# Scores of two heads in one two-bank tile, in a decoder step of attention, state space and MLP layers

## The chip, the cores and the metric

The kernel runs on one core of a Trainium2 chip. The metric is the device time of one execution in microseconds, as the median of several runs; a profiled execution gives the trace that is read here. The core has a matrix engine (TensorE, PE in the rows, with its weight loads as PEld), a vector engine (DVE), an activation engine (ACT), GpSimd (POOL) and a sync engine (SP); SP and POOL issue most transfers.

## The reference

One step of a trunk of two layers is computed for two groups with the same weights: a prompt of 512 rows without past, and a sample of 8 sequences of 8 rows, each with 2,048 cached keys and values per head. The first layer is stick-breaking attention with 16 heads of 64, the second a diagonal state-space layer; each is followed by an MLP with a convolution. For the change only the attention of the prompt counts:

```python
z = einsum("bqhd,bkhd->bhqk", q, k) * HEAD_DIM ** -0.5 + bias[h]
causal = k_pos < q_pos
log_keep = where(causal, log_sigmoid(-z), 0)
between = cumsum(log_keep, reverse) - log_keep
weights = where(causal, exp(log_sigmoid(z) + between), 0)
out = einsum("bhqk,bkhd->bqhd", weights, v)
```

The kernel computes it in products: the running product of sigmoid(-z) from the right, times sigmoid(z).

## The kernel before

The prompt's 512 rows are four tiles of 128 rows (NT = 4). Heads are handled in pairs: the 128 columns of a pair c are head 2c (partitions 0 to 63 once transposed) and head 2c + 1 (partitions 64 to 127).

The loop at L786 to L797 runs over c from 0 to 9, with three stages of different pairs in each turn. `project_pair` computes keys and values of pair c by matmuls of 256 columns (L266 to L268, psg). `norm_pair` (L631) normalizes queries and keys of pair c - 1 and transposes them on TensorE into PSUM tiles pqk (L651), which ACT and DVE copy to qkT. `prompt_pair` (L661) does the attention of pair c - 2. In turns 8 and 9 there is no projection.

A fourth stream of work, `sample_cache`, reads 64 pairs of cache pages per run. A step of it is 1 MB of keys (kp, issued on POOL, turned by DVE at L427), 1 MB of values (vp, issued on SP), 32 passes of scores (z, L448), sigmoids and scans, two transposes (L473) and 16 passes of value sums (po, L483). It yields four times per step. After the stream the sample's own new rows follow (`sample_new`: zn at L522, pon at L559), then its output projection (pso), and then the sample joins the prompt in the MLP.

How these are woven: `tick(cycles)` is called where matmuls are issued. Each companion (the stream with a period of 2,400 cycles, `norm_pair` with 6,000, `prompt_pair` with 1,200) is advanced by one yield when its period is used up; a companion doesn't count its own ticks. That gives the order in which instructions are written down. The framework then arranges them for each engine by that priority and by when they can be ready, with a modelled time, and each engine runs its own list strictly in that arranged order. So an instruction of later priority may stand ahead of one that would have to wait.

In `prompt_pair` an item is one row tile i and one head e. For each item: one score matmul (L674; float32, two passes each with its own weight load), a mask matmul in bfloat16 onto the diagonal block (L675), two sigmoids on ACT (L678, L679), a scan and a product on DVE (L681, L682). One item later its weights are transposed back into the same PSUM tile z (L691) and copied by ACT to pwT (L693). Two items later, for both heads of a row, the value sums go into poT (L704). The tiles z and pqk share two PSUM buffers of one bank each (tag "pz", PZ = 2). The tiles pleft, psg and pwT have two buffers each. PSUM's eight banks are taken: two for pz, two for the projections, one for poT, three for the stream.

Of the kernel before, what the change touches and what calls it, by code (L numbers as in the profile page):

```python
# [9 lines left out]
F32 = mybir.dt.float32  # L10
# [3 lines left out]
AF = mybir.ActivationFunctionType  # L14
# [3 lines left out]
P = 128  # L18
D = 1024
KC = D // P  # L20
SEQ = 512
NT = SEQ // P
# [5 lines left out]
HD = 64  # L28
# [21 lines left out]
PZ, PG = 2, 2  # L50
# [40 lines left out]
def hybrid_kernel(  # L91
# [9 lines left out]
    V, S, G, T, SP = nc.vector, nc.scalar, nc.gpsimd, nc.tensor, nc.sync  # L101
# [10 lines left out]
    ident = const.tile([P, P], F32, name="ident")  # L112
# [184 lines left out]
    def attention_layer(sp, sps):  # L297
# [333 lines left out]
        def norm_pair(pool, psp, c, k, v):  # L631
# [14 lines left out]
            out = []  # L646
            for m in range(2):
                yield
                ps = psp.tile([P, SEQ], F32, name="pqk", tag="pz", bufs=PZ)
                for i in range(NT):  # L650
                    T.transpose(ps[:, i * P:(i + 1) * P], k[:, i] if m else q_all[:, c, i], ident)  # L651
                a = pool.tile([P, SEQ], F32, name="qkT", tag=f"qkT{m}")
                if m:
                    V.tensor_copy(a, ps)
                else:
                    S.activation(a, ps, AF.Copy, scale=qgT)
                out.append(a)
# [3 lines left out]
        def prompt_pair(pool, psp, c, qT, kT, v):  # L661

            po = psp.tile([P, SEQ], F32, name="poT", tag="poT", bufs=1)
            items = [(i, e) for i in range(NT) for e in range(2)]
            live = {}
            for x in range(len(items) + 2):
                if x < len(items):
                    i, e = items[x]
                    nk = (i + 1) * P
                    h = 2 * c + e  # L670
                    r = slice(e * HD, e * HD + HD)

                    z = psp.tile([P, SEQ], F32, name="pz", tag="pz", bufs=PZ)
                    T.matmul(z[:, :nk], qT[r, i * P:nk], kT[r, :nk], start=True, stop=False)  # L674
                    T.matmul(z[:, i * P:nk], ident_b, mask_b, start=False, stop=True)  # L675
                    left = pool.tile([P, SEQ], F32, name="pleft", tag="pleft", bufs=B1)
                    sg = pool.tile([P, SEQ], F32, name="psg", tag="psg", bufs=B2)
                    S.activation(left[:, :nk], z[:, :nk], AF.Sigmoid, bias=nbias_h[:, h:h + 1], scale=-0.125)  # L678
                    S.activation(sg[:, :nk], z[:, :nk], AF.Sigmoid, bias=bias_h[:, h:h + 1], scale=0.125)  # L679
                    back = left[:, :nk][:, ::-1]  # L680
                    V.tensor_tensor_scan(back, back, back, 1.0, ALU.mult, ALU.min)  # L681
                    V.tensor_tensor(sg[:, :nk - 1], sg[:, :nk - 1], left[:, 1:nk], ALU.mult)  # L682
                    live[x] = z, sg
                    tick(4 * nk + P)
                    yield
                if x - 1 in live:
                    z, sg = live[x - 1]
                    i = items[x - 1][0]
                    nk = (i + 1) * P
                    for kb in range(i + 1):  # L690
                        T.transpose(z[:, kb * P:(kb + 1) * P], sg[:, kb * P:(kb + 1) * P], ident)  # L691
                    wT = pool.tile([P, SEQ], F32, name="pwT", tag="pwT", bufs=B3)
                    S.copy(wT[:, :nk], z[:, :nk])  # L693
                    live[x - 1] = wT
                    tick(2 * nk)
                    yield
                if x - 2 in live and x % 2:

                    i = items[x - 2][0]
                    wTs = [live.pop(y) for y in (x - 3, x - 2)]  # L700
# [6 lines left out]
                    yield  # L707
# [3 lines left out]
        with pool_(name="start", bufs=2) as wp, pool_(name="start_ps", bufs=5, space=PSUM) as psp:  # L711
# [9 lines left out]
            with tc.high_priority():  # L721
# [4 lines left out]
                for n in range(2):  # L726
                    ps = bank()
# [1036 lines left out]
```

## Time and profile before

| | us |
|---|---|
| median of three runs | 1748.3 |
| lowest and highest of them | 1742.35, 1749.19 |
| profiled execution | 1757.19 |
| its span, first to last instruction | 1755.2 |
| TensorE busy in it | 1657.5 (94%) |
| DVE busy | 1156.4 (66%) |
| ACT busy | 739.3 (42%) |
| GpSimd busy | 379.0 (22%) |

TensorE's mean granted clock was 0.976 of full speed, and 297.4 MB were moved in the span, 169 GB/s on average, over 300 GB/s while the cache is streamed. Busy shares over the whole span mix stages with different limits, so a stage is read by itself: busy time of each engine, granted clock and DMA share in its window, then what ends the waits there.

### The profile page before, as it was taken

How to read it: one execution, taken by the hardware profiler on the slowest of the kernel's cores; microseconds unless marked ns; L12 is line 12 of the kernel's file. 1: busy time of each engine (PE TensorE's matmuls, PEld its weight loads, DVE VectorE, ACT ScalarE, POOL GpSimd, SP SyncE). 2: the span in 40 equal slices, each digit the busy share in tenths (PEclk: the TensorE clock that was granted, in tenths of full speed). 3: DMA queues.
4: the chain of work that ended last, by engine and by line, in shares of the span. 5: the costliest groups of instructions: out<-in, count | busy, mean ns of one | idle time of the engine just before them, and what ended most of it. 6: DMA issues, size and time to landing. Idle time of an engine off the chain costs nothing. (4 is left out here: it accounts for less than half of the span.)

```text
span 1755.2 us, 34213 instructions
## 1 busy us (share of the span) xinstructions
PE 1657.5 (94%) x12765; PEld 1405.2 (80%) x12765; DVE 1156.4 (66%) x2132; ACT 739.3 (42%) x1526; POOL 379.0 (22%) x583
## 2 busy tenths in 40 slices
PE   5999999999898899989998999999999999999999
PEld 4877776665577769868898897898889989999897
DVE  8377888888778668977687777655456444444343
ACT  4344555555533643323445354544434323323231
POOL 4032333332332002652242330111101001000000
PEclk8999999998899999989999999999999999999999
DMA  8299989898798444234757364544322222222221
GB/s 272 72 313 316 316 284 340 288 344 287 253 346 292 147 131 124 96 110 110 163 147 188 117 170 123 156 163 137 103 69 83 81 85 85 82 77 86 82 87 56
DMA packets 278714, 297.44 MB, mean 169 GB/s; under 512 B 70808, under 2 KB 214129, under 8 KB 278548
## 3 DMA queue, kind: packets, MB, share of 16 engines
q1 hardware_dynamic: 240210, 226.65, 41.8%
q0 software_dynamic: 37184, 67.55, 11.2%
q8 instruction: 101, 1.65, 0.4%
q10 hardware_dynamic: 1154, 1.05, 0.2%
q14 instruction: 65, 0.53, 0.1%
HBM read 268.93 MB, written 26.13 MB: 168 GB/s over the span
## 5 line engine op out<-in xcount | busy, mean ns | idle before, releaser
L139 DVE TENSOR_TENSOR wlo<-raw,whi 128x1024 fp32r<-128x1024 f32 x203 | 255.6, 1261 | 256.2 <-ACT whi L138 241.3
L880 PE MATMUL up<-hT,whi 128*128 128x256 f32 (+2 forms) x1344 | 408.0, 304 | 12.0 <-DVE gf L1000 6.3
L881 PE MATMUL up<-hT,whi 128*128 128x256 f32 (+2 forms) x1344 | 403.9, 301 | 0.0
L882 PE MATMUL up<-hT,wlo 128*128 128x256 f32 (+2 forms) x1344 | 403.8, 301 | 0.0
L138 ACT CAST whi<-raw 128x1024 fp32r<-128x1024 f32 x206 | 215.4, 1049 | 337.7 <-PE up L881 155.3
L880 PEld LDWEIGHTS up<-hT,whi 128*128 128x128 f32 x1344 | 257.9, 192 | 21.5 <-DVE gf L1000 8.0
L881 PEld LDWEIGHTS up<-hT,whi 128*128 128x128 f32 x1344 | 258.0, 192 | 3.5 <-issue 0.8
L882 PEld LDWEIGHTS up<-hT,wlo 128*128 128x128 f32 x1344 | 257.6, 192 | 1.3
L415 POOL DMA_DIRECT2D kp<-in_cache_k_dram x256 | 166.1, 649 | 360.8 <-DVE kt L427 190.9
L427 DVE STREAM_TRANSPOSE kt<-kp 128x1024 f32<-128x1024 f32 x128 | 152.1, 1222 | 42.2 <-DMA kp<-in_cache_k_dram 20.6
L986 POOL COPY cst<-apad 128x2 f32<-128x2 f32 x44 | 39.0, 885 | 517.2 <-ACT apad L974 517.2
L266 PE MATMUL dn<-whi,g 128*128 128x512 f32 x352 | 136.9, 399 | 7.8 <-DVE xres L1077 5.0
L267 PE MATMUL dn<-wlo,g 128*128 128x512 f32 x352 | 140.5, 399 | 0.0
L268 PE MATMUL dn<-whi,g 128*128 128x512 f32 x352 | 139.1, 398 | 0.0
L266 PE MATMUL psg<-whi,hT 128*128 128x256 f32 (+1 forms) x320 | 100.7, 317 | 0.1
L267 PE MATMUL psg<-wlo,hT 128*128 128x256 f32 (+1 forms) x320 | 99.3, 311 | 0.0
L268 PE MATMUL psg<-whi,hT 128*128 128x256 f32 (+1 forms) x320 | 98.0, 309 | 0.0
L457 ACT ACTIVATE left<-z,nbias_r 128x128 f32<-128x128 f32 x128 | 40.3, 367 | 111.1 <-PE z L448 109.9
L266 PEld LDWEIGHTS dn<-whi,g 128*128 128x128 f32 x352 | 66.1, 189 | 24.6 <-DVE xres L1077 5.5
L483 PE MATMUL po<-vp,wT 128*32 128x256 f32 x1024 | 73.4, 404 | 9.5 <-DMA vp<-in_cache_v_dram 7.3
L268 PEld LDWEIGHTS dn<-whi,g 128*128 128x128 f32 x352 | 66.5, 189 | 15.5 <-DVE g L1016 0.3
L267 PEld LDWEIGHTS dn<-wlo,g 128*128 128x128 f32 x352 | 66.6, 189 | 15.3
(484 smaller groups left out, 3291.4 us busy)
## 6 DMA issues: line engine op xcount, KB each, us to landing
kp<-in_cache_k_dram POOLq DMA_DIRECT2D x256, 256.0 KB, 6.5
vp<-in_cache_v_dram SPq DMA_DIRECT2D x128, 512.0 KB, 7.0
raw<-in_ffn_w_up_dram SPq DMA_DIRECT2D x96, 512.0 KB, 4.4
raw<-in_ffn_w_down_dram SPq DMA_DIRECT2D x48, 512.0 KB, 3.3
raw<-in_attn_w_qkv_dram SPq DMA_DIRECT2D x64, 128.0 KB, 6.4
raw<-in_attn_w_o_dram SPq DMA_DIRECT2D x16, 512.0 KB, 5.4
raw<-in_ssm_w_glu_dram SPq DMA_DIRECT2D x32, 256.0 KB, 3.1
f_scr<-ca SPq DMA_DIRECT2D x8, 512.0 KB
```

The lines of the kernel that those rows point to most:

```text
L138: S.copy(hi, src)
L139: eng.tensor_tensor(lo, src, hi.bitcast(F32), ALU.subtract)
L266: T.matmul(ps, x[0], whi, start=st, stop=False)
L267: T.matmul(ps, x[0], wlo, start=False, stop=False)
L268: T.matmul(ps, x[1], whi, start=False, stop=sp_)
L415: last_dma[G] = G.dma_start(kps[i][32 * x:32 * x + 32], page[j])
L427: V.transpose(kts[i, a].rearrange("p b c k -> p b (c k)"), kps[i][:, :, a * 256:(a + 1) * 256])
L457: S.activation(left[:, a, :P], z[:, a * P:(a + 1) * P], AF.Sigmoid, bias=nbias_r[:, a:a + 1], scale=-0.125)
L483: T.matmul(po[32 * h:32 * h + 32, a].rearrange("p (s j d) -> p s j d", s=2, j=2), wT[:, a, 32 * h:32 * h + 32], v[:, a, h], start=m0 == NP ...
L880: T.matmul(ps[:, :t1 - t0], w[0][:, k, :], hi, start=k == 0, stop=False)
L881: T.matmul(ps[:, :t1 - t0], w[0][:, k, :], lo, start=False, stop=False)
L882: last_mm["PE"] = T.matmul(ps[:, :t1 - t0], w[1][:, k, :], hi, start=False, stop=k == KC - 1)
```

## The change

The two one-bank buffers of the tag "pz" become one buffer of two banks, a tile of 128 x 2 x 512. In `norm_pair` queries and keys are transposed into the two halves of one such tile, with one yield ahead of both in place of one ahead of each. In `prompt_pair` the loop goes over row tiles: the score matmuls of both heads are issued one behind the other, then both masks, then sigmoids, scan and product of each head, then after three yields (with the value sums of the row before between them) the transposes and copies of both heads. The ticks of a row were 2 x (4 nk + 128) + 2 x 2 nk + 4 nk, with nk = 128 (i + 1), and are now (4 nk + 256) + 4 nk + 4 nk. Nothing else changes.

```diff
--- before.py
+++ after.py
@@ -47,7 +47,7 @@
 ASTEPS, AEND = 44, 20
 SSTART = 14
 GROUPS = [[4], [0, 1], [2, 3]]
-PZ, PG = 2, 2
+PG = 2
 LAG = 19000
 GLAG = 6
 GT = 3
@@ -644,16 +644,16 @@
             with tc.high_priority():
                 SP.dma_start(k_out[:, c * P:(c + 1) * P].rearrange("(i p) f -> p i f", p=P), k)
             out = []
+            yield
+            ps = psp.tile([P, 2, SEQ], F32, name="pqk", tag="pz", bufs=1)
             for m in range(2):
-                yield
-                ps = psp.tile([P, SEQ], F32, name="pqk", tag="pz", bufs=PZ)
                 for i in range(NT):
-                    T.transpose(ps[:, i * P:(i + 1) * P], k[:, i] if m else q_all[:, c, i], ident)
+                    T.transpose(ps[:, m, i * P:(i + 1) * P], k[:, i] if m else q_all[:, c, i], ident)
                 a = pool.tile([P, SEQ], F32, name="qkT", tag=f"qkT{m}")
                 if m:
-                    V.tensor_copy(a, ps)
+                    V.tensor_copy(a, ps[:, m])
                 else:
-                    S.activation(a, ps, AF.Copy, scale=qgT)
+                    S.activation(a, ps[:, m], AF.Copy, scale=qgT)
                 out.append(a)
             ready[c] = *out, v
             yield
@@ -661,50 +661,53 @@
         def prompt_pair(pool, psp, c, qT, kT, v):
 
             po = psp.tile([P, SEQ], F32, name="poT", tag="poT", bufs=1)
-            items = [(i, e) for i in range(NT) for e in range(2)]
-            live = {}
-            for x in range(len(items) + 2):
-                if x < len(items):
-                    i, e = items[x]
-                    nk = (i + 1) * P
+            sums = None
+            for i in range(NT):
+                nk = (i + 1) * P
+
+                z = psp.tile([P, 2, SEQ], F32, name="pz", tag="pz", bufs=1)
+                for e in range(2):
+                    r = slice(e * HD, e * HD + HD)
+                    T.matmul(z[:, e, :nk], qT[r, i * P:nk], kT[r, :nk], start=True, stop=False)
+                for e in range(2):
+                    T.matmul(z[:, e, i * P:nk], ident_b, mask_b, start=False, stop=True)
+                sgs = []
+                for e in range(2):
                     h = 2 * c + e
-                    r = slice(e * HD, e * HD + HD)
-
-                    z = psp.tile([P, SEQ], F32, name="pz", tag="pz", bufs=PZ)
-                    T.matmul(z[:, :nk], qT[r, i * P:nk], kT[r, :nk], start=True, stop=False)
-                    T.matmul(z[:, i * P:nk], ident_b, mask_b, start=False, stop=True)
                     left = pool.tile([P, SEQ], F32, name="pleft", tag="pleft", bufs=B1)
                     sg = pool.tile([P, SEQ], F32, name="psg", tag="psg", bufs=B2)
-                    S.activation(left[:, :nk], z[:, :nk], AF.Sigmoid, bias=nbias_h[:, h:h + 1], scale=-0.125)
-                    S.activation(sg[:, :nk], z[:, :nk], AF.Sigmoid, bias=bias_h[:, h:h + 1], scale=0.125)
+                    S.activation(left[:, :nk], z[:, e, :nk], AF.Sigmoid, bias=nbias_h[:, h:h + 1], scale=-0.125)
+                    S.activation(sg[:, :nk], z[:, e, :nk], AF.Sigmoid, bias=bias_h[:, h:h + 1], scale=0.125)
                     back = left[:, :nk][:, ::-1]
                     V.tensor_tensor_scan(back, back, back, 1.0, ALU.mult, ALU.min)
                     V.tensor_tensor(sg[:, :nk - 1], sg[:, :nk - 1], left[:, 1:nk], ALU.mult)
-                    live[x] = z, sg
-                    tick(4 * nk + P)
-                    yield
-                if x - 1 in live:
-                    z, sg = live[x - 1]
-                    i = items[x - 1][0]
-                    nk = (i + 1) * P
+                    sgs.append(sg)
+                tick(4 * nk + 2 * P)
+                yield
+                if sums:
+                    sums()
+                yield
+                yield
+                wTs = []
+                for e, sg in enumerate(sgs):
                     for kb in range(i + 1):
-                        T.transpose(z[:, kb * P:(kb + 1) * P], sg[:, kb * P:(kb + 1) * P], ident)
+                        T.transpose(z[:, e, kb * P:(kb + 1) * P], sg[:, kb * P:(kb + 1) * P], ident)
                     wT = pool.tile([P, SEQ], F32, name="pwT", tag="pwT", bufs=B3)
-                    S.copy(wT[:, :nk], z[:, :nk])
-                    live[x - 1] = wT
-                    tick(2 * nk)
-                    yield
-                if x - 2 in live and x % 2:
-
-                    i = items[x - 2][0]
-                    wTs = [live.pop(y) for y in (x - 3, x - 2)]
+                    S.copy(wT[:, :nk], z[:, e, :nk])
+                    wTs.append(wT)
+                tick(4 * nk)
+                yield
+
+                def sums(i=i, wTs=wTs):
+
                     for kb in range(i + 1):
                         for e, wT in enumerate(wTs):
                             r = slice(e * HD, e * HD + HD)
                             T.matmul(po[r, i * P:(i + 1) * P], v[:, kb, r], wT[:, kb * P:(kb + 1) * P],
                                      start=kb == 0, stop=kb == i)
                     tick(4 * (i + 1) * P)
-                    yield
+            sums()
+            yield
             S.copy(q_all[:, c].rearrange("p i f -> p (i f)"), po)
 
         xT = columns_tile()
```

## Rows read from the trace of the kernel before

**Rows 1.** Stages: window, busy us and instructions per engine, TensorE clock, DMA share, GB/s.
```profile
130.00:412.00 282.00, 270.77 (x3038) 194.98 (x3037) 234.21 (x438) 152.85 (x422) 90.72 (x140) 0.98 0.92 314
412.00:482.00 70.00, 61.93 (x629) 35.33 (x628) 52.46 (x88) 37.52 (x102) 23.33 (x36) 0.85 0.80 261
482.00:548.00 66.00, 65.95 (x653) 49.37 (x651) 54.24 (x104) 28.76 (x73) 23.10 (x36) 1.00 0.94 322
```

**Rows 2.** Waits of TensorE, 130 to 482 us: us in total, times, longest.
```profile
PE pz L674 <- ACT pwT L693: 5.3, 5, 2.1
PE po L483 <- DMA vp<-in_cache_v_dram: 3.3, 3, 1.9
```

**Rows 3.** Stream's score passes (L448) by window: busy us (count), clock, DMA share, GB/s.
```profile
83.00:124.00 41.00, 8.48 (x224) 0.96 0.79 265
130.00:412.00 282.00, 41.59 (x1120) 0.98 0.92 314
412.00:482.00 70.00, 12.51 (x288) 0.85 0.80 261
482.00:575.00 93.00, 12.75 (x384) 0.96 0.92 311
```

**Rows 4.** Timeline of TensorE where the sample joins: start, us, instruction, idle before.
```profile
647.23 0.79 PE L263 MATMUL pso<-whi,soT 128*128 128x512 f32 x1 [4.36 <-DVE srow L275]
```

**Rows 5.** Timeline of TensorE: scores of 512 and 128 columns and what follows them.
```profile
315.41 1.12 PE L674 MATMUL pz<-qkT 64*128 64x512 f32 x2
316.47 0.23 PE L675 MATMUL pz<-mask_b,ident_b 128*128 128x128 bf16 x1
...
318.32 1.07 PE L483 MATMUL po<-vp,wT 128*32 128x256 f32 x16
319.32 1.12 PE L674 MATMUL pz<-qkT 64*128 64x512 f32 x2
...
323.29 0.48 PE L674 MATMUL pz<-qkT 64*128 64x128 f32 x2
323.71 0.23 PE L675 MATMUL pz<-mask_b,ident_b 128*128 128x128 bf16 x1
```

**Rows 6.** Timeline: 32 passes of 128 rows, 32 of 64; then pon by itself (ns).
```profile
317.18 1.08 PE L448 MATMUL z<-kt,Qall 128*32 128x128 f32 x32
...
618.62 0.77 PE L559 MATMUL pon<-nkv,nwork 64*32 64x128 f32 x32
...
L559 PE MATMUL pon<-nkv,nwork x64: 266/269/293, 618.6 to 625.9; 64*32 64x128 f32 x64
```

**Rows 7.** Timeline of all engines: the last row of the seventh pair.
```profile
436.15 1.12 PE L674 MATMUL pz<-qkT 64*128 64x512 f32 x2 [0.84 <-ACT pwT L693]
438.10 1.12 PE L674 MATMUL pz<-qkT 64*128 64x512 f32 x2
438.60 1.18 DVE L681 TENSOR_TENSOR_SCAN pleft<-pleft 128x512 f32<-128x512 f32 x1
441.28 1.27 DVE L682 TENSOR_TENSOR psg<-psg,pleft 128x511 f32<-128x511 f32 x2
443.14 1.09 ACT L693 COPY pwT<-pz 128x512 f32<-128x512 f32 x2
444.16 0.48 PE L674 MATMUL pz<-qkT 64*128 64x128 f32 x2
```

**Rows 8.** The score tile by line: ns min/median/max, first and last start.
```profile
L691 PE MATMUL pz<-ident,psg x160: 270/273/475, 151.2 to 476.8; 128*128 128x128 f32 x160
L674 PE MATMUL pz<-qkT x128: 272/482/1219, 143.1 to 468.3; 64*128 64x128 f32 x32, 64*128 64x256 f32 x32, 64*128 64x384 f32 x32, 64*128 64x512 f32 x32
```

**Rows 9.** Timeline of one item beside the projections: its score, what follows, its copy.
```profile
308.63 0.91 PE L674 MATMUL pz<-qkT 64*128 64x384 f32 x2
309.46 0.41 PE L448 MATMUL z<-kt,Qall 128*32 128x128 f32 x5
...
318.14 0.50 ACT L693 COPY pwT<-pz 128x384 f32<-128x384 f32 x1
```

## The prediction

> **What bounds the kernel now.** I read the busy time by stage first. From 130 to 412 us the projections of keys and values, the prompt's attention and the cache stream of the sample run woven into one another: TensorE is busy 270.8 of 282 us, DVE 234.2, and the DMA engines have a share of 0.92. From 412 to 482 us the last two head pairs run with no projection beside them, and TensorE is busy 61.9 of 70 us at a mean clock of 0.85. From 482 on come the output projection, and from about 548 the first MLP chunks, with the rest of the stream [rows 1]. Second, the waits of TensorE from 130 to 482 us: the longest group is a score that waits for the copy which frees its PSUM tile, 5.3 us; data of the stream cost it 3.3 us [rows 2]. So up to 412 us TensorE is the bound, by a small margin over the transfers. Third, the pace of the stream, counted by its score matmuls, 32 to a step: 7 steps in the 41 us from 83 on, then 35 in 282 us (8.1 us each), 9 in 70 us, 12 in 93 us [rows 3]. The 5.9 us of the first stretch show that the stream can go faster than it does later. Last the place where the sample joins the prompt: at 647.2 us TensorE has sat idle for 4.4 us waiting for the sample's rows [rows 4]. That chain starts when the stream ends, so an attention that ends earlier is worth its whole gain only if the stream ends earlier as well.
>
> **The change part by part.**
>
> *Scores side by side.* A score of one head reads 64 partitions: head 0 the lower, head 1 the upper half. Now each is issued alone and a mask matmul follows. From the start of a score to the start of its mask it is 0.42 us for 128 columns and 1.06 us for 512 [rows 5]; that is 0.21 us per 128 columns and 0.21 us on top, so 0.63 and 0.85 us for the widths between. A head pair has one score of each width and head: 2 x 2.96 us. In the new order head 1's score follows head 0's at once, on the other half of the array's rows and in another bank. Does this trace show two row halves at work together? Yes, in the sample's own rows: 32 passes of 64 rows and 128 columns, half of them on each row half and into two PSUM tiles, take 0.77 us from the first start to the last end. The same number of passes of 128 columns with all 128 rows, on the same four column groups, take 1.08 us [rows 6]. A single pass shows as 0.27 us long (the least of its group) and, with 0.21 us per 128 columns in two passes, a round of four starts every 0.11 us, so the eight rounds of the second kind need 7 x 0.11 + 0.27 = 1.05 us; 0.77 us is room for five and a half rounds, and so rounds of the two row halves ran at the same time. I therefore take the second score as free, 2.96 us per pair; the other bound is no gain at all.
>
> The Trainium skill speaks against the full value here: "TensorE: Matmul & The Clock Gate", Part 3, reports 3.07 times for four row tiles of 512 columns, that is 77% of the ideal. By that share two row tiles would give 1.53 times, and an estimate by the page is 2.05 us per pair in place of 2.96, or 14 us in place of 20.8 in the sum below. No row here shows such a loss.
>
> *Where that lies.* Six pairs lie before 412 us, where TensorE is the bound: 6 x 2.96 = 17.8 us on the path. In the last two pairs a row of the score matrix is a chain: the first score of the last row at 436.15, the other head's at 438.10, a scan of 1.18 us per head, two products of 1.27 us together, the last copies of both heads from 443.14 to 444.23 [rows 7]. Both heads share DVE, so of 2 x 2.96 us I count half: 3.0 us. Sum 20.8 us.
>
> *One tile of two banks in place of two tiles of one.* No bank more or less, no instruction more. But row i+1 can't begin its scores until both heads of row i are copied out; before, each head's tile came free by itself. In the last two pairs this is so already (444.16, the next pair's first score, comes with the end of the last copy). Beside the projections it isn't: there the tile's hold is covered by projection matmuls, and costs nothing as long as a row takes less than its share of the pair's time; if that cover is gone it is the slower rival below. Taken: 0; bounds -3 us (the score waits of 5.3 us shrink) and +32 us.
>
> *Transposes of queries and keys.* The same eight transposes and two copies; they take the shared tile once, not twice, and one hand-over falls away. They are free when norms are ready. Taken as 0, within 1 us per pair either way. The DMA of k_out is issued before, from the same place in SP's queue; no queue is passed by.
>
> *Ticks.* The stream, the norm work and the attention advance by counted cycles. A pair ticked 16 nk + 256 per row, now 12 nk + 256; nk sums to 1,280, so 21,504 becomes 16,384. Over eight pairs that is 40,960 cycles, 17 turns of 2,400, a little over four of the stream's 64 steps that are due later. The trace shows how much of it matters: by the ticks 50 steps were due at 412 us and 54 at 482, but done were 43 and 52, one of them between 124 and 130 us [rows 3]. The order already runs behind what is due. With the change 47 and 50 are due, so only the last stretch is cut, by some two steps. A step costs TensorE 1.19 us of scores (41.59 over 35) [rows 3], 1.00 us of value sums (318.32 to 319.32) [rows 5] and two transposes, 2.5 us in all: 5 us leave the attention stage and come back in the stage behind it. That is no gain in TensorE's work, but it delays the stream by 2 x 7.75 us = 15.5 us against the attention's end.
>
> *The sum.* The attention ends 20.8 + 5 = 25.8 us earlier. The stream's end comes 25.8 - 15.5 = 10.3 us earlier, if its pace afterwards stays; with the DMA share at 0.94 from 482 to 548 us [rows 1] I don't expect it to quicken much. TensorE's work up to the join falls by 20.8 us. Since TensorE already waits at the join [rows 4], the stream's end is the nearer of the two: I take 13 us. After the join nothing changes. The profiled execution took 1757.2 us (span 1755.2); the sum gives 1744. The median of the runs shown is 1748.3, 8.9 us under that execution; on its scale the forecast is 1735.
>
> **The rivals.**
>
> *The stream sets the end (no change).* The order of instructions follows the stream's pace, and what TensorE saves becomes idle time before the join. For it: 8 us per step in three stretches of very different content [rows 3], the DMA share of 0.92 and 0.94 [rows 1], and the wait at the join [rows 4]. Against it: 5.9 us per step at the start [rows 3] and only 3.3 us of TensorE's waits for stream data in 352 us [rows 2]. Gain 0 to 5 us: 1746.
>
> *One tile makes the row the bound (slower).* Now the eight pairs go from 143.1 to 477 us [rows 8], 41.8 us per pair; TensorE alone would allow 38.8 with the change. Four rows share one tile, so it decides from a row of 9.7 us on. A single head beside the projections has taken 10.0 us from its score at 308.63 to the end of its copy at 318.64 [rows 9]; the second head of the row would add its scan and product, some 1.8 us [rows 7]. If every row took 11.8 us, a pair would take 47.2, six pairs 32 us longer than now. At 11 us a pair takes 44: 2.2 us more in six pairs, 13 us, 1761. Against it: the row without cover took 8.1 us [rows 7], and in the narrower rows the DVE part is far smaller. The Trainium skill names the same danger ("TensorEngine Tiling (Array Packing)", Performance Considerations): packing speeds up the matmuls and not the emptying of PSUM, which may become the bottleneck. Here emptying is what frees the tile.
>
> *It doesn't do what it says.* The order is made by priority and readiness, and other matmuls come between: a score of 308.63 us is followed by scores of the stream before its mask [rows 9]. If the two scores are parted, or the row halves take turns, only the shift of ticks is left: 1747.
>
> *More than the sum.* The stream quickens too (5.9 us were seen), and the slow clock and idle time from 412 to 482 us (8.1 us) shrink: 30 us, 1718.
>
> **How the numbers follow.** Forecast 0.48, with a range of its own from 1723 to 1742; the stream sets the end 0.22; one tile makes the row the bound 0.17; not side by side 0.07; more than the sum 0.06. Two runs differ by up to 0.4% here, and 0.5%, 8.7 us, is about what can be told from no change: faster means under 1739.6, slower over 1757.0. Faster: most of the forecast (0.42), all of the last case and a little of the second (0.04): 0.52. Slower: the row-bound case but for its mild part: 0.15. The rest, 0.33, is the same. The range of eight in ten goes from 1718, the largest gain, to 1760, nearly the middle of the slower rival.
>
> **What would show it.** Side by side: the second score of a row starts some ns behind the first, and from the first to the first mask it is about 1.06 us for 512 columns. The row: from first score to last copy under 9.7 us beside the projections. The attention's end: the last transposes of scores at about 451 us where they were at 477. The stream: about 50 steps done by then. The join: the wait at the sample's output projection tells whether the stream's end decides; a long idle there (15 us and more) means the first rival. The prediction is wrong if TensorE's waits for the copies of the score tile grow from 5 us to tens of us, or if the join stays at 647 us.

## The result, and the profile after

The changed kernel takes 1790.69 us (median of four runs, 1788.94 to 1795.5); the kernel before, run beside it, 1747.82 us (1742.35 to 1749.19). The ratio is 1.0234, with a 95% interval from 1.0202 to 1.0267. The change makes the kernel 43 us slower; the forecast was 13 us faster, and 1790.69 lies above the range.

The profiled execution took 1790.86 us (span 1789.0), as long as the median. The profiled execution of before was 9 us over its median, so the two traces differ by 34 us only; where in that execution the 9 us went, the trace alone can't tell. Every comparison with the trace of before below is off by up to that much.

First the busy time by stage, the view of [rows 1]: window, length, then busy us and instructions of PE, PEld, DVE, ACT and POOL, granted clock, DMA share, GB/s. The last two windows go from 130 us to the first pass of the sample's output projection (pso), here at 664.5 us.

```profile
130.00:412.00 282.00, 246.63 (x2962) 179.25 (x2965) 219.41 (x408) 136.18 (x387) 93.54 (x145) 0.95 0.92 316
412.00:482.00 70.00, 54.00 (x657) 34.77 (x652) 55.16 (x100) 35.14 (x99) 25.69 (x40) 0.84 0.90 319
482.00:548.00 66.00, 52.95 (x636) 29.24 (x629) 52.06 (x84) 32.57 (x89) 20.74 (x32) 0.86 0.85 287
130.00:664.50 534.50, 465.09 (x5048) 336.07 (x5048) 403.11 (x774) 257.14 (x680) 143.84 (x228) 0.93 0.79 267
```

The same last window of before, up to its first pso pass at 636.2 us:

```profile
130.00:636.20 506.20, 476.08 (x5065) 343.95 (x5064) 400.51 (x773) 258.44 (x680) 144.63 (x228) 0.96 0.84 283
```

This is the account of the change. From 130 us to that pass TensorE works 11.0 us less (465.1 for 476.1), and sits idle 39.3 us more (69.4 for 30.1); so the pass comes 28.3 us later. TensorE's mean clock in that window is 0.93, and 0.96 in before; at the lower clock the same work takes longer (three transposes take 0.88 us at 340.63 in the piece below, where the granted clock is half, and 0.55 us at 344.43, where it is full), so the 11.0 us are less than the work saved (20.9 us by e4). No engine has taken TensorE's place as the busy one: from 130 to 412 us DVE falls from 234 to 219 us and ACT from 153 to 136, and the granted clock falls from 0.98 to 0.95. Behind the pass little changes: to the end of the span it is 1124.5 us, 1119.0 in before, and between 1121.8 and 1127.6 in all the experiments below, so the 5.5 us that make up the 34 us lie within what the runs spread there.

Second the score tile by line, the view of [rows 8] (ns least, median, greatest; first and last start):

```profile
L694 PE MATMUL pz<-ident,psg x160: 270/273/477, 150.0 to 547.1; 128*128 128x128 f32 x160
L671 PE MATMUL pz<-qkT x128: 272/482/1116, 142.4 to 535.0; 64*128 64x128 f32 x32, 64*128 64x256 f32 x32, 64*128 64x384 f32 x32, 64*128 64x512 f32 x32
```

The eight pairs now go from 142.4 to 548 us, 50.7 us per pair, where they took 41.8. The last transposes start at 547.1 us, not at 476.8 as before, nor at 451 as forecast.

Third the timeline of a piece of the fourth pair: start, us, engine, line, instruction; in brackets the idle time before and what ended it. Lines of other work are left out.

```profile
335.84 0.92 PE L671 MATMUL pz<-qkT 64*128 64x384 f32 x4
336.69 0.29 PE L673 MATMUL pz<-mask_b,ident_b 128*128 128x128 bf16 x2
...
339.95 1.00 DVE L683 TENSOR_TENSOR psg<-psg,pleft 128x383 f32<-128x383 f32 x2
340.63 0.88 PE L694 MATMUL pz<-ident,psg 128*128 128x128 f32 x3 [3.07 <-ACT wT L475]
341.43 1.94 PE L483 MATMUL po<-vp,wT 128*32 128x256 f32 x16
...
343.14 1.35 PE L448 MATMUL z<-kt,Qall 128*32 128x128 f32 x32
...
344.43 0.55 PE L694 MATMUL pz<-ident,psg 128*128 128x128 f32 x3
345.59 0.50 ACT L696 COPY pwT<-pz 128x384 f32<-128x384 f32 x1
347.05 0.66 PE L651 MATMUL pqk<-ident,q_all 128*128 128x128 f32 x4
...
350.74 0.67 DVE L654 COPY qkT<-pqk 128x512 f32<-128x512 f32 x1
351.61 1.13 PE L671 MATMUL pz<-qkT 64*128 64x512 f32 x4
```

One tile, one holder after the other. The row of 384 columns holds it from its scores at 335.84 us to the end of head 1's copy at 346.09, 10.25 us. Then the transposes of queries and keys of the next pair hold it until 351.41 us, and 0.2 us later the next row begins. The 24 rows of the first six pairs took 6.5 to 17.3 us each, 10.6 on average (253.4 us in all); the other 67.4 us of these pairs' 320.8 us lie between rows, 35.0 of them in the six gaps in which pqk has the tile. That is 13.4 us per row, and 53.5 us per pair, beside the projections.

A good part of the 10.6 us is not the row's own work. In the piece shown the second product ends at 340.95 us, but head 1's transposes start at 344.43, behind value sums and scores of the stream (L483, L448), which stand ahead of them in TensorE's order. On average over the 24 rows, by the same starts and ends, the masks are through after 1.1 us, the last sigmoid after 3.0, the last product after 6.6; head 1's transposes start after 9.5. Even the rows of 128 columns among them were held 8 to 11 us. (The bracket at 340.63 names a copy of the stream; the transposes need head 0's product, and it ended within 0.2 us of that copy.)

In the first lines both scores are seen side by side: `x4` is two passes of each head, and the masks of both follow 0.85 us after the first score's start. That is what one score of this width was worked out to take before.

Fourth what TensorE, and then ACT, waited for (us in total, times, longest), the view of [rows 2]; TensorE from 130 to 548 us, ACT from 130 to 550:

```profile
PE pz L694 <- DVE psg L683: 22.7, 13, 9.7
PE po L483 <- DMA vp<-in_cache_v_dram: 8.6, 4, 3.3
PE z L473 <- DVE sg L464: 8.6, 2, 4.8
...
PE pz L671 <- ACT pwT L696: 0.2, 1, 0.2
...
ACT pwT L696 <- PE pz L694: 52.1, 33, 7.8
```

The same groups in before, TensorE's from 130 to 548 us, ACT's from 130 to 482:

```profile
PE z L473 <- DVE sg L464: 2.3, 3, 1.2
...
PE pz L691 <- DVE psg L682: 1.8, 3, 0.9
...
ACT pwT L693 <- PE pz L691: 17.9, 19, 2.6
```

TensorE's new wait lies inside the row: the transposes wait for the product of the same row, 22.7 us for 1.8, since no other row's scores may be in flight. That is 20.9 of the 39.3 us more that it is idle; the stream's own waits grew too, for its data 8.6 us (3.3 in [rows 2]) and for its products (L464) 8.6 us for 2.3. Scores that wait for the copy that frees the tile, 5.3 us in [rows 2], have fallen to 0.2 us: in the arranged order the score just stands later.

Fifth the cover. Three stretches of the changed kernel, first with all instructions, then with those of the projections (L266, the first of their three lines) alone (PE, PEld, clock, DMA share, GB/s):

```profile
221.40:255.60 34.20, 27.34 (x394) 16.64 (x393) 26.84 (x45) 18.16 (x53) 12.96 (x20) 0.90 0.94 319
280.20:313.30 33.10, 26.05 (x315) 14.78 (x314) 24.06 (x37) 15.40 (x43) 12.17 (x19) 0.90 0.89 300
334.80:372.90 38.10, 25.32 (x329) 15.30 (x328) 24.77 (x49) 16.02 (x45) 10.79 (x18) 0.82 0.74 249
...
221.40:255.60 34.20, 0.27 (x1) 0.07 (x1) 0.90 0.94 319
280.20:313.30 33.10, 0.12 (x1) 0.00 (x0) 0.90 0.89 300
334.80:372.90 38.10, 0.00 (x0) 0.00 (x0) 0.82 0.74 249
```

A turn of the loop ends only when its attention is through, so a turn whose attention is late runs out of projection matmuls. Such stretches lasted at most 20.1 us in before (266.2 to 286.3); here they last 33 to 38 us, and 26.7 us of the 35.4 us that TensorE is idle from 130 to 412 us lie in these three. Between and behind them, with projections, TensorE is busy 23.5 of 24.6 us, 21.5 of 21.5 and 38.0 of 39.1.

### The profile page after: what moved, and what is told of

Same layout as the page of the kernel before. It is cut to its first block, busy times and chain, and to the rows that moved or that the text cites. A ratio compares the mean times of both kernels' runs of the same rounds, so it can differ in the third digit from the quotient of the medians.

```text
span 1789.0 us, 34229 instructions
## 1 busy us (share of the span) xinstructions
PE 1649.0 (92%) x12765; PEld 1399.8 (78%) x12765; DVE 1161.0 (65%) x2132; ACT 737.6 (41%) x1524; POOL 378.5 (21%) x583
## 5 line engine op out<-in xcount | busy, mean ns | idle before, releaser
L266 PE MATMUL dn<-whi,g 128*128 128x512 f32 x352 | 137.9, 402 | 7.8 <-DVE xres L1080 5.0
L266 PE MATMUL psg<-whi,hT 128*128 128x256 f32 (+1 forms) x320 | 100.2, 315 | 0.0
L483 PE MATMUL po<-vp,wT 128*32 128x256 f32 x1024 | 79.8, 425 | 16.5 <-DMA vp<-in_cache_v_dram 10.7
L448 PE MATMUL z<-kt,Qall 128*32 128x128 f32 x2048 | 85.5, 294 | 7.5 <-DVE kt L427 6.5
L266 PEld LDWEIGHTS dn<-whi,g 128*128 128x128 f32 x352 | 66.9, 191 | 24.9 <-DVE xres L1080 5.5
L448 PEld LDWEIGHTS z<-kt,Qall 128*32 128x32 f32 x2048 | 59.5, 117 | 28.9 <-DVE kt L427 9.5
```

Source lines behind the costliest of these rows:

```text
L266: T.matmul(ps, x[0], whi, start=st, stop=False)
L448: T.matmul(z[32 * h:32 * h + 32, a * P:(a + 1) * P].rearrange("p (c k a) -> p k a c", c=4, k=4), Qall[:, b, 8 * a + 2 * h + half, :], kt[: ...
L483: T.matmul(po[32 * h:32 * h + 32, a].rearrange("p (s j d) -> p s j d", s=2, j=2), wT[:, a, 32 * h:32 * h + 32], v[:, a, h], start=m0 == NP ...
```

## The experiments

Three theories were told apart. A: the one tile makes each row's life, from score to copy, the bound of the attention. B: the three yields between sigmoids and transposes, which the new order of the loop brings, stretch each row. C: the smaller ticks hold the stream back. Each ratio below is against runs of the kernel before on the same chip, and a hundredth is 17.5 us. The table goes with all of them; the second to fifth column are of the profiled execution: the start of the last copy of poT (the attention's end), the first pso pass, and TensorE's busy and idle time from 130 us to that pass. A profiled execution can lie off its kernel's median, as those of before (9 us over it) and of e5 (12.6 us over it) do. The diffs show the lines that carry an edit; lines that only follow from it, and edits named as another run's, are left out.

| kernel | attention's end | first pso | busy | idle | ratio (95%) |
|---|---|---|---|---|---|
| before | 479.6 | 636.2 | 476.1 | 30.1 | 1 |
| after | 549.9 | 664.5 | 465.1 | 69.4 | 1.0234 (1.0202, 1.0267) |
| e1_two_tiles | 476.8 | 634.1 | 472.8 | 31.3 | 1.0072 (1.0033, 1.0110) |
| e2_no_scan_after | 493.8 | 635.5 | 461.3 | 44.2 | 1.0065 (1.0045, 1.0086) |
| e3_no_scan_before | 449.1 | 622.9 | 470.2 | 22.7 | 0.9946 (0.9925, 0.9966) |
| e4_parted | 566.7 | 681.2 | 486.0 | 65.2 | 1.0379 (1.0339, 1.0418) |
| e5_one_bank_less | 565.8 | 680.2 | 479.8 | 70.4 | 1.0240 (1.0196, 1.0283) |
| e6_qk_own_bank | 516.1 | 655.5 | 470.7 | 54.8 | 1.0161 (1.0128, 1.0195) |
| e7_three_tiles | 461.0 | 620.6 | 471.0 | 19.6 | 0.9962 (0.9943, 0.9981) |
| e8_no_yields | 545.0 | 659.3 | 460.3 | 69.0 | 1.0200 (1.0160, 1.0241) |
| e9_before_three | 461.9 | 626.3 | 474.2 | 22.1 | 0.9988 (0.9963, 1.0012) |
| e10_old_ticks | 554.2 | 675.9 | 467.4 | 78.5 | 1.0280 (1.0245, 1.0315) |
| e11_early_release | 455.5 | 612.0 | 455.6 | 26.4 | 0.9942 (0.9918, 0.9966) |
| e12_early_release_sg | 456.4 | 618.6 | 457.2 | 31.4 | 0.9975 (0.9954, 0.9996) |
| e13_early_parted | 485.6 | 644.7 | 486.0 | 28.7 | 1.0071 (1.0045, 1.0097) |
| e14_before_early | 468.4 | 631.7 | 478.0 | 23.7 | 1.0001 (0.9986, 1.0016) |

### Is it the one tile, the order or the ticks?

**e1_two_tiles**: the changed kernel, with its new loop and ticks, but on the old two buffers of one bank.

```diff
-                z = psp.tile([P, 2, SEQ], F32, name="pz", tag="pz", bufs=1)
+                z = [psp.tile([P, SEQ], F32, name="pz", tag="pz", bufs=2) for e in range(2)]
-            ps = psp.tile([P, 2, SEQ], F32, name="pqk", tag="pz", bufs=1)
             for m in range(2):
+                ps = psp.tile([P, SEQ], F32, name="pqk", tag="pz", bufs=2)
```

> The changed kernel, in its new written order, but with two PSUM tiles of one bank in place of one of two banks, for the scores and for the queries and keys: each head's tile comes free by itself. Theory A (the shared tile makes the row of both heads a serial chain and that bounds the attention): nearly all of the 43 us comes back, 1750 to 1760 us, and the last copy of the last pair moves from 548 us to about 490. Theory B (the new written order, with three yields between scores and transposes, makes the rows late): it stays at 1785 to 1795. Theory C (the smaller ticks put the stream back): it stays at 1785 to 1795.

The attention ends at 476.8 us again and the added idle time is gone (31.3 us); the ratio falls from 1.0234 to 1.0072, 28 of the 41 us by ratios (1762.0 us, 2 us above what theory A expected). The one tile is the cause of most of the loss. Here each score goes when its own tile is free, only 5 of the 32 score pairs stand next to each other (31 of 32 in the changed kernel), and so the gain is lost with the loss. The 0.0072 that stay, 13 us, are what the new loop and its ticks cost on two tiles; no run parts them further. The row of e1:

```profile
L711 ACT COPY q_all<-poT x8: 586/586/603, 190.0 to 476.8; 128x512 f32<-128x512 f32 x8
```

**e2_no_scan_after, e3_no_scan_before**: the scan and the product of DVE left out, in the changed kernel and in that of before. It shortens every row's life.

```diff
-                    V.tensor_tensor_scan(back, back, back, 1.0, ALU.mult, ALU.min)
-                    V.tensor_tensor(sg[:, :nk - 1], sg[:, :nk - 1], left[:, 1:nk], ALU.mult)
```

> The changed kernel without the scan and the product on DVE of the prompt's attention (its weights are then the plain sigmoids): some 2.6 us of DVE work per row of two heads are left out of the chain from scores to transposes, 32 rows. Theory A: the chain of 32 rows shortens by up to 83 us, the attention ends at TensorE's own pace, 65 us or more earlier, and the time falls by 40 us or more, to 1750 or below. Theory B and C: DVE is not what the rows wait for, and the time falls by less than 15 us.

> The kernel before with the same work left out (scan and product of the prompt's attention). It measures how much of e2 is the chain of the shared tile. Theory A: before, the two tiles cover this work, TensorE is the bound, and the time falls by no more than 15 us, to 1733 or above; so e2 gains at least 25 us more than e3. Theory B and C: e2 and e3 gain the same within 10 us.

By ratios the changed kernel gains 30 us (1.0065 for 1.0234), that of before 9 us (0.9946); the difference, 20 us, is what the same cut is worth only because the tile is held. That is more than B or C allow and less than A expected: the direction is A's, its size was put too high. e3 shows why: an attention that ends 30.5 us earlier (449.1 for 479.6) brings the pso pass 13.3 us earlier, and the median 9 us. What the attention gains or loses reaches the join only in part, 44% there; in the changed kernel it was 28.3 of 70.3 us, 40%.

**e8_no_yields**: the changed kernel without the two yields behind the value sums.

```diff
                 if sums:
                     sums()
-                yield
-                yield
```

> The changed kernel without the two yields behind the value sums, so the transposes of a row are written down one yield behind its scores instead of three (two without sums). Theory B (the written order makes the rows late): the time falls by 15 us or more. Theory A (the rows are late against the written order anyway, and wait for the tile): within 10 us of 1790.7.

6 us come back (1.0200), less than the two intervals can tell from nothing, and TensorE's idle time stays (69.0 us). B falls: the yields are a small part at most.

**e10_old_ticks**: the changed kernel with the ticks per row of before.

```diff
-                tick(4 * nk + 2 * P)
+                tick(8 * nk + 2 * P)
```

> The changed kernel with the ticks of a row as they were (16 nk + 256), so as much of the stream is due by the attention's end as before. Theory C (the ticks): the time falls by 10 us or more. Theory A: within 8 us of 1790.7.

1.0280, 8 us slower than the change by ratios, and idle time of 78.5 us. C falls: the time doesn't go down. Whether it goes up isn't clear, since the two intervals overlap.

### What side by side is worth

**e4_parted**: the changed kernel, with each mask directly behind its own score, so that the two scores don't meet.

```diff
                 for e in range(2):
                     T.matmul(z[:, e, :nk], qT[r, i * P:nk], kT[r, :nk], start=True, stop=False)
-                for e in range(2):
                     T.matmul(z[:, e, i * P:nk], ident_b, mask_b, start=False, stop=True)
```

> The changed kernel with each head's mask matmul directly behind its score, so the two scores no longer lie side by side. One tile of two banks, yields and ticks as in the change. It prices the side-by-side issue by itself. If the two scores run together as read (2.96 us per pair less on TensorE) and the row chain is the bound: each row gets longer by one score and the time rises by 10 to 24 us, to 1800 to 1815. If they gave nothing: within 5 us of 1790.7.

1.0379: the parted scores cost 25 us more, and TensorE is busy 20.9 us longer up to the pso pass (486.0 for 465.1), with about the same idle time. First a row of the changed kernel, then one of e4, 512 columns each:

```profile
453.38 1.13 PE L671 MATMUL pz<-qkT 64*128 64x512 f32 x4 [0.85 <-DVE qkT L654]
454.45 0.28 PE L673 MATMUL pz<-mask_b,ident_b 128*128 128x128 bf16 x2
```

```profile
518.30 1.12 PE L671 MATMUL pz<-qkT 64*128 64x512 f32 x2
519.36 0.23 PE L672 MATMUL pz<-mask_b,ident_b 128*128 128x128 bf16 x1
519.52 1.12 PE L671 MATMUL pz<-qkT 64*128 64x512 f32 x2
520.57 0.23 PE L672 MATMUL pz<-mask_b,ident_b 128*128 128x128 bf16 x1
```

Counted from the first score's start, the masks of both heads are through after 1.35 us side by side and after 2.50 us parted. So the change did what it says, and its gain is in the 1790.69 us already.

### Who holds the tile

These kernels need a bank. It is taken from the projections, which go through the row tiles singly with one bank for psg.

**e5_one_bank_less**: the changed kernel with that alone.

```diff
-GROUPS = [[4], [0, 1], [2, 3]]
-PG = 2
+GROUPS = [[4], [0], [1], [2], [3]]
+PG = 1
```

> Control for the next two: the changed kernel with one PSUM bank for the projections of keys and values in place of two, one row tile per group in place of two, so one bank is spare and unused. Every theory: the projections' bank changes hands 40 times without a second one, which costs nothing while the attention's rows are behind anyway and up to 25 us where they aren't: 1790 to 1815.

1.0240: no difference that can be told from the change. Its profiled execution, 1807.84 us, is the longest of its four runs, so its row of the table lies high.

**e6_qk_own_bank**: e5, and queries and keys transposed in the bank that came free.

```diff
-            ps = psp.tile([P, 2, SEQ], F32, name="pqk", tag="pz", bufs=1)
             for m in range(2):
+                ps = psp.tile([P, SEQ], F32, name="pqk", tag="pq", bufs=1)
```

> As e5, and the spare bank takes the transposed queries and keys, one after the other; the tile of two banks is the scores' alone. In the changed kernel's trace the rows of a pair stand apart by 3 to 9 us where queries and keys hold the tile, eight times. If that hold is a large part of theory A: the attention ends 25 to 48 us earlier than in e5 and the time is 15 to 30 us lower than e5. If the rows' own chain is all of it: within 8 us of e5.

1.0161: 14 us less than e5 by ratios, a little under what was expected. The attention ends 49.7 us earlier than in e5's long execution, and 33.8 us earlier than in the changed kernel's, 4.2 us per pair. So pqk in the score tile is a good part of the tile's hold.

**e7_three_tiles**: e5's banks, and scores and pqk in three buffers of one bank (the edit of e1 with `bufs=3`).

> As e5, with three tiles of one bank for scores, queries and keys in place of one tile of two banks: a head's tile is free by itself, and there is one more. Theory A: faster than e5 by 30 us or more and no slower than the two tiles of e1 by more than what e5 lost against the change. Theories B and C: within 10 us of e5.

0.9962, 49 us below e5. A score waits for a copy once, 0.8 us, and TensorE's idle time is 19.6 us, the least of all; but only 4 of 32 score pairs are adjacent, and busy time is 471.0 us.

**e9_before_three**: the kernel before with the same three buffers.

```diff
-GROUPS = [[4], [0, 1], [2, 3]]
-PZ, PG = 2, 2
+GROUPS = [[4], [0], [1], [2], [3]]
+PZ, PG = 3, 1
```

> The kernel before, in its old written order, with the banks of e7: one for the projections, three tiles of one bank for scores, queries and keys. It tells what in e7 the third tile gave. If the third tile is all of it: 1740 to 1748, as e7. If the new order with both heads' scores behind one another gives something by itself once the tile isn't shared: 1749 to 1756.

0.9988, and 1 lies in the interval: in the old order a third buffer is worth nothing that can be told. From e7 it can't be told either, as the intervals overlap.

**e11_early_release**: e6, and the weights of each head are transposed back into the bank of pqk, no longer into the score tile. The score tile is then free as soon as the sigmoids have read it.

```diff
                 for e, sg in enumerate(sgs):
+                    zt = psp.tile([P, SEQ], F32, name="pzT", tag="pq", bufs=1)
                     for kb in range(i + 1):
-                        T.transpose(z[:, e, kb * P:(kb + 1) * P], sg[:, kb * P:(kb + 1) * P], ident)
+                        T.transpose(zt[:, kb * P:(kb + 1) * P], sg[:, kb * P:(kb + 1) * P], ident)
-                    S.copy(wT[:, :nk], z[:, e, :nk])
+                    S.copy(wT[:, :nk], zt[:, :nk])
```

> The changed kernel with its tile of two banks for the scores alone, given back after the sigmoids: the transposed weights of each head, and the queries and keys, go through one other bank, taken from the projections as in e5. All scores stay side by side. Theory A: the tile is held some 4 us of a row's 10, the rows overlap again and the attention ends by 480 us or earlier: 1738 to 1755. If side by side itself were harmful, or the written order were the cause: 1775 or more.

0.9942: 10 us below the kernel before and 51 us below the changed one by medians (1739.5 us, eight runs). Up to the pso pass it has the least busy time of all, 455.6 us, and 26.4 us of idle time, less than the kernel before: it keeps the gain and not the loss. A piece of its timeline, and its first stage:

```profile
332.29 0.62 ACT L680 ACTIVATE psg<-pz,bias_h 128x384 f32<-128x384 f32 x1
...
333.71 1.13 PE L671 MATMUL pz<-qkT 64*128 64x512 f32 x4
334.77 0.28 PE L673 MATMUL pz<-mask_b,ident_b 128*128 128x128 bf16 x2
...
340.43 0.55 PE L695 MATMUL pzT<-ident,psg 128*128 128x128 f32 x3
```

```profile
130.00:412.00 282.00, 273.17 (x3294) 199.96 (x3296) 246.98 (x472) 162.51 (x455) 98.50 (x152) 0.99 0.97 334
```

The scores of the next row (512 columns) start 0.8 us behind the last sigmoid of the row of 384, and 6.7 us before that row's first transposes. In the changed kernel they had to come behind its last copy. TensorE is busy 273 of 282 us again, at a clock of 0.99. From the scores to the last sigmoid the tile is held 7.4 us on average in the first 24 rows (1.9 to 17.8), not the 4 us expected, and these rows come 10.1 us apart for the changed kernel's 13.4.

**e12_early_release_sg**: e11 with four buffers of psg in place of two (`B2 = 4`), for products that wait for the transposes.

> As e11 with four buffers in place of two for the weights of a head between product and transposes, so the sigmoids of the next row needn't wait for the transposes of this one. If that wait is what is left of the chain: 5 us or more below e11. If not: within 4 us of e11.

0.9975, no better than e11: 6 us above it by ratios, where the intervals overlap. The tile is held 4.7 us on average for 7.4, but the attention ends where it did (456.4 us): the hold no longer sets the pace, and the buffers of psg don't bind.

**e13_early_parted**: e11 with the edit of e4.

> e11 with each head's mask behind its own score, so the scores don't lie side by side. If side by side saves what the prediction's sum took (20.8 us of TensorE on the path, of which the stream passes a third to a half on): 7 to 14 us above e11, 1747 to 1754. If it gives nothing where the tile isn't the bound: within 4 us of e11.

1.0071: where the tile isn't the bound, side by side is worth 0.0129, 23 us by ratios, and 30.4 us of TensorE's busy time up to the pso pass (part of it the clock, 0.96 for 0.98 on average in that window). More than was expected of it.

**e14_before_early**: the order of before with e11's banks, that is with transposes and pqk in a bank of their own and two tiles for scores.

```diff
-PZ, PG = 2, 2
+PZ, PG = 2, 1
-                ps = psp.tile([P, SEQ], F32, name="pqk", tag="pz", bufs=PZ)
+                ps = psp.tile([P, SEQ], F32, name="pqk", tag="pq", bufs=1)
+                    zt = psp.tile([P, SEQ], F32, name="pzT", tag="pq", bufs=1)
```

> The kernel before, in its old order, with the banks of e11: two tiles of one bank for scores, given back after the sigmoids; transposed weights, queries and keys through one other bank; one bank for the projections. If the early release is what e11 gained: 1736 to 1743. If side by side is: 1746 to 1755.

1.0001. The early release alone gives nothing, so e11's gain needs the two scores side by side. And e13 is 0.0070 above e14: the tile of two banks and the new loop cost 12 us even when the tile is given back early. The three ratios make one sum: 23 us for side by side, less 12 us, are the 10 us by which e11 is below e14. e1 lies 13 us over before with two tiles of one bank, so these 12 us need not be the two-bank tile's.

## Why the prediction was wrong

**Scores side by side: right.** 2.96 us per pair, 23.7 us in eight pairs, was the estimate of the work saved; e4 shows 20.9 us of it. The row of 512 columns has both scores in 1.07 us where [rows 5] have 1.06 us for one. The share that was weighed against it, from "TensorE: Matmul & The Clock Gate", Part 3 of the Trainium skill (3.07 times for four row tiles), would have made this 2 x 1.06 / 1.53 = 1.39 us as an estimate; for two row tiles the trace doesn't agree with that estimate, and four weren't run.

**Where that lies: it did not apply.** The gain was put on the path because TensorE was the bound up to 412 us [rows 1]. In the changed kernel it no longer is: it works 246.6 of these 282 us. Where the tile goes back early TensorE is busy again, and there side by side was worth 23 us of the time (e13 less e11).

**One tile of two banks in place of two tiles of one: the step that failed.** It was taken at 0, on the ground that projection matmuls cover the hold of the tile "as long as a row takes less than its share of the pair's time", 9.7 us. The one item looked at beside the projections [rows 9] was already above that for a single head (and from 314.5 us on no projection stood beside it), and the row of 8.1 us that was set against it is one without cover [rows 7]. The trace of before holds more: its first 24 rows took 5.4 to 24.2 us from the first head's score to the end of the second head's copy, 12.5 on average, and a single head 7.8. (The second head starts later there.) Two tiles let such rows overlap; with one they can't. Measured in the changed kernel: 10.6 us on average. It is the slower rival, with its own decision point, and its mechanism is shown by e1 (two tiles: the idle time goes), e2 less e3 (a shorter row: 20 us) and e11 (a shorter hold: all of it comes back). What was said against the rival, that the narrow rows have far less DVE work, didn't count: much of a row's hold is waiting, and rows of 128 columns were held 9.4 us on average.

**The rival's price was mis-sized too,** 13 us for 43. Its term was 4 x 11 = 44 us per pair for the row alone, in six pairs; the first six pairs took 53.5 us each. The 11 us for a row's life was good. What it left out lies between the rows, 2.8 us each, and 11.2 us per pair: the tile is also pqk's (35.0 us in six pairs), and each hand-over costs (the other 32.4). The bound of +32 us that stood beside the 0 was on the attention's end, and fell short as well: that end came 70.3 us later.

**Transposes of queries and keys: wrong.** They were taken at 0, within 1 us per pair, since one hand-over falls away. But with one tile no score can be in flight while both transposes and their two copies are made: 347.05 to 351.41 us in the timeline above. Against e5 a bank of their own is worth 14 us of the time (e6), and against the changed kernel's own profile 4.2 us of the attention's end per pair. With two tiles [rows 8] there was a second one for the attention meanwhile.

**Ticks: the count was right, its effect wasn't.** The stream was to fall back by two steps. The score passes of the stream, the view of [rows 3]:

```profile
130.00:412.00 282.00, 47.52 (x1177) 0.95 0.92 316
412.00:482.00 70.00, 14.06 (x304) 0.84 0.90 319
482.00:548.00 66.00, 14.52 (x319) 0.86 0.85 287
```

1,177 passes from 130 to 412 us where there were 1,120, and by 548 us the stream's scores are all but done, which took until about 573 us before. With an attention that takes 70 us longer, it overtook. Against e10 the cut itself is worth 8 us or nothing.

**The sum.** "The stream's end is the nearer of the two" doesn't fit the changed kernel: its attention ends last, at 550 us, behind a stream whose scores are through (24 of its value sums are left, the last at 599.2 us). From the attention's end to the pso pass, first in the changed kernel and then in before:

```profile
550.50:664.50 114.00, 109.11 (x781) 91.34 (x774) 74.87 (x178) 51.24 (x100) 3.87 (x12) 0.99 0.34 103
480.20:636.20 156.00, 144.99 (x1407) 114.86 (x1408) 115.64 (x251) 69.88 (x162) 31.02 (x53) 0.96 0.71 236
```

In both it is TensorE's own work that fills the time. In before 384 score passes and 224 value sums of the stream are part of it; in the changed kernel nearly all of that had been done beside the longer attention, and so the join comes 28 us later and not 70. Of an attention that ends earlier half was to reach the join (13 of 25.8 us): 44% did in e3, and 40% of the loss did in the changed kernel. The share came out, by luck: the reason given for it, a stream that falls back by two steps, did not.

**The signs.** The side-by-side start, the 9.7 us and the last transposes told what they were named for. At the join TensorE waited 2.4 us, for 4.4 in [rows 4], so the long idle of the rival in which the stream sets the end wasn't there. The wait of TensorE for the copies of the score tile, which was to grow if the prediction was wrong, didn't: the idle time came up one step earlier in the row, where the transposes wait for the product. Since the order is arranged ahead, a buffer that is short need not show as a wait for its release.

**What stays open.** Where the 9 us of the profiled execution of before lie. Why the share that passes is 40 to 44% and not another. That the long stretches without projections make the idle time, rather than only coincide with it, is argued from the loop's structure and was not tried; e11, whose tile goes back early, has such a stretch too (388.0 to 457.4 us), and TensorE is idle 14.5 us in it. And of the 12 us that e13 costs over e14, how much is the tile, how much the new loop and how much its ticks.

## What to carry to other kernels

Matmuls that are to run side by side need their banks at the same time, and a tile of both is given back only when its slower half is: work out the time from first write to last read of it, add every other user of the tag, and compare that with the pace that the stage needs, before the saving is counted. Measure the hold over many rows of the trace, with the same work beside them, since much of it can be waiting. If it is over, shorten the hold: a tile that goes free at its first readers, with later steps in another bank, turned +2.3% into -0.6% here. Three tiles of one bank in place of the pair's gave -0.4%, which can't be told from it, but without the scores side by side. And where an order is arranged ahead, look for a shortage of buffers in the pace of the tile and in idle time inside its chain, not only in waits for its release.

## What the runs showed of the hardware

Two float32 matmuls of 64 rows and 512 columns, on the two halves of the array's rows and into two banks, took 1.07 us together; one alone took 1.06 us. No part of the second was seen in the time, up to the start of the matmul that follows.
